# Output product of the last two tokens by tokens on TensorE, with ScalarE's functions grouped and the decay mask on GpSimd, in a hybrid mLSTM and retention block

## The chip, the cores and the metric

The kernel runs on one core of a Trainium2 chip, in one launch. The metric is the device time of that launch in microseconds (us). The engines are named as the profile names them: PE (TensorE's matmuls; PEld its weight loads), DVE (VectorE), ACT (ScalarE), POOL (GpSimd) and SP (SyncE, which issues most DMAs).

## What is computed

One block of a language model over 16 meta tokens and 1024 frames, D = 1024, in f32. A token mixer with eight heads of 256 value columns (four mLSTM heads, four retention heads) is followed by a gated MLP with a causal convolution. Cut to what the change touches:

```python
def token_mixer(u, w_in, ml_conv_w, ml_b_i, ml_b_f, ml_norm_g, rt_norm_g, w_out):
    ...
    qk = jax.nn.silu(causal_dwconv(jnp.concatenate([ml_q, ml_k], axis=-1), ml_conv_w))
    ...
    h_ml = mlstm_chunkwise(to_chunks(q), to_chunks(k), to_chunks(v),
                           to_chunks(li[..., None])[..., 0], to_chunks(lf[..., None])[..., 0])
    h_ml = head_norm(from_chunks(h_ml), ml_norm_g).reshape(b, lp, ML_HEADS * ML_DV)
    h_ml = jax.nn.sigmoid(ml_o.astype(jnp.float32)) * h_ml
    ...
    h_rt = head_norm(from_chunks(h_rt), rt_norm_g).reshape(b, lp, RT_HEADS * RT_DV)
    h_rt = jax.nn.silu(rt_g.astype(jnp.float32)) * h_rt
    mixed = jnp.concatenate([h_ml, h_rt], axis=-1).astype(u.dtype)
    return (mixed @ w_out)[:, n_pad:]
```

In the mLSTM heads a score is weighted with exp(log_d - m_row), where log_d is minus infinity above the diagonal: that is the mask. Four functions of ScalarE alternate: Silu (q and k of mLSTM heads, gate of retention heads), Exp (the decays of mLSTM heads), Sigmoid (gate of mLSTM heads) and Sqrt (the norms).

## The kernel before

Features lie on the 128 partitions and tokens along the free axis, 1040 of them in pieces of 400, 384 and 256 tokens, or in nine chunks (16, then eight of 128) for the scan. Products in the projections are made of three fp32r matmuls each (high by high, high by low, low by high): a weight tile lands by DMA in a raw buffer (two buffers, tag "raw"), ACT casts it to a high part (L151), DVE takes the low part as the rest (L152), and then the buffer is free for the next DMA in the list of units. The order of that list for one head is o (two tiles), m (two tiles of w_out for the last two tokens, of the head before), v (two tiles), q and k of the next head.

The heads run in the order 4, 0, 1, 2, 3, 5, 6, 7 (L1003). For each head the loop merges the gate projections `po` (o_group, L422, three pieces by two halves) with the first chunks of the scan, then the value projections `pv` of the next head (v_group, L358) with the other chunks and the normalisation (post_steps, L872), and then comes the next head's q and k (`pq`, `pk`, qk_group, L395). scan_a (L789) makes the scores and `kwh`, the weighted k for the state update; scan_b (L827) makes the update `u`, the state `C` and the numerator `n`. Before the merged loops of a head, tables (L518) fetches its decays from DRAM into A1 and A2, adds the mask to A1 on DVE (L532, L533) and makes nine Exps on ACT (L536). ACT loads a table (ACT_TABLE_LOAD) whenever the next function is in another set.

The normalised and gated output of a head goes to DRAM (`mxd`), except for the last two tokens of 1040: these go to the small tile mm, since the output stage (class Seven, L579, a scheme with seven half-size products in place of eight, bank names `pwx` and `pwy`) works on 1024 tokens. Their product with w_out is made by last_two (L176) on DVE: for each of the 16 tiles of w_out and each of the two tokens one instruction multiplies the tile with a per-partition value and adds it to acc, 128 partitions by 1024. The sum over partitions is taken much later, in step "4" of the output stage, with 16 matmuls of one column each (L1189), after which DVE adds the result to resid. Sums of weight blocks for the seven products are made by DMAs that add in DRAM (wsum, L188): a first pair on SP's queue (L194), a chain of five on POOL's (L196).

PSUM has eight banks of [128, 512] f32: three "pp", two "sA", one each of "num", "upd" and "tr" (L109). The transposes of post_steps go to "tr", one bank for each half.

The order in which each engine gets its instructions is decided by a scheduler at build time, which may interleave what the program writes one after another; on the chip each engine keeps that order. A call `after(x, y)` adds an edge that only orders x behind y.

## Time and profile before

| | |
|---|---|
| median of 3 runs (lowest, highest) | 1543.4 us (1542.33, 1548.02) |
| the profiled execution's own time | 1549.12 us |
| its span, first to last instruction | 1547.3 us |
| mean granted clock of TensorE | 0.991 |
| heads 4 and 0 to 3, from about | 86 to 500 us |
| heads 5, 6, 7, to about | 742 us |
| output stage (seven products) | 700 to 936 us |
| gated MLP, up and gate, then down | 936 to 1300, 1300 to 1520 us |

A row of a timeline reads: start, duration, engine, line, operation, output tile <- input tiles, shape, and in brackets how long the engine sat idle before it and what ended that. Matmuls are pipelined, so the time that one costs is the step from its start to the next one's start, not its own duration. A granted clock of 0.50 in a stretch means that TensorE ran at half speed there. In the groups of lines the columns behind the bar are busy time, mean duration in ns, and idle time before with what ended it.

### The profile page before, as it was taken

How to read it: one execution, taken by the hardware profiler on the slowest of the kernel's cores; microseconds unless marked ns; L12 is line 12 of the kernel's file. 1: busy time of each engine (PE TensorE's matmuls, PEld its weight loads, DVE VectorE, ACT ScalarE, POOL GpSimd, SP SyncE). 2: the span in 40 equal slices, each digit the busy share in tenths (PEclk: the TensorE clock that was granted, in tenths of full speed). 3: DMA queues.
4: the chain of work that ended last, by engine and by line, in shares of the span. 5: the costliest groups of instructions: out<-in, count | busy, mean ns of one | idle time of the engine just before them, and what ended most of it. 6: DMA issues, size and time to landing. Idle time of an engine off the chain costs nothing.

```text
span 1547.3 us, 25387 instructions
## 1 busy us (share of the span) xinstructions
PE 1524.0 (98%) x9763; PEld 1400.5 (91%) x9763; DVE 1090.0 (70%) x2342; ACT 739.3 (48%) x1494; POOL 90.6 (6%) x109
## 2 busy tenths in 40 slices
PE   8999999999999999999999999999999999999997
PEld 7989999999999999997788998999999999888887
DVE  8757767676867566668867778666666666778657
ACT  7365555555543434336454555444444444434443
POOL 0001000010101000000000000211111110000000
PEclk9999999999999999999999999999999999999999
DMA  6124344262648152347542327888656567923213
GB/s 215 42 70 122 77 123 90 98 142 79 161 111 197 54 128 71 101 111 244 185 137 92 96 94 244 211 223 200 161 145 161 148 156 197 373 99 113 96 41 109
DMA packets 105192, 213.41 MB, mean 138 GB/s; under 512 B 9384, under 2 KB 31600, under 8 KB 105072
## 3 DMA queue, kind: packets, MB, share of 16 engines
q1 hardware_dynamic: 86384, 176.86, 33.6%
q0 software_dynamic: 18544, 34.87, 15.1%
q8 instruction: 76, 1.25, 0.3%
q14 instruction: 44, 0.36, 0.1%
q10 hardware_dynamic: 144, 0.07, 0.0%
HBM read 182.37 MB, written 84.19 MB: 172 GB/s over the span
## 4 chain that ended last, share of the span: by engine, by line
PE 93%; DMA 2%; DVE 2%; ACT 2%; issue 1%; SPq 0%; DVEq 0%; ACTq 0%
PE pv L378 4%; PE pv L379 4%; PE pv L380 4%; PE po L388 3%; PE po L390 3%; PE po L389 3%; PE pdx L554 3%; PE pdx L556 3%; PE pdx L555 3%; PE pup_x L555 2%; PE pup_x L556 2%; PE pga_x L554 2%; PE pga_x L556 2%; PE pga_x L555 2%; PE pup_x L554 2%; PE pwx L555 2%
## 5 line engine op out<-in xcount | busy, mean ns | idle before, releaser
L378 PE MATMUL pv<-hi_v,uh 128*128 128x256 f32 (+1 forms) x512 | 148.3, 290 | 3.1 <-ACT hi_v L151 2.1
L379 PE MATMUL pv<-lo_v,uh 128*128 128x256 f32 (+1 forms) x512 | 147.3, 288 | 0.0
L380 PE MATMUL pv<-hi_v,ul 128*128 128x256 f32 (+1 forms) x512 | 146.2, 287 | 0.0
L388 PE MATMUL po<-uh,hi_o 128*128 128x386 f32 (+2 forms) x384 | 123.9, 323 | 1.1 <-DVE kT L419 1.1
L389 PE MATMUL po<-ul,hi_o 128*128 128x386 f32 (+2 forms) x384 | 122.7, 319 | 0.0
L390 PE MATMUL po<-uh,lo_o 128*128 128x386 f32 (+2 forms) x384 | 122.6, 319 | 0.0
L378 PEld LDWEIGHTS pv<-hi_v,uh 128*128 128x128 f32 x512 | 98.2, 192 | 6.5 <-issue 2.9
L379 PEld LDWEIGHTS pv<-lo_v,uh 128*128 128x128 f32 x512 | 98.2, 192 | 0.8 <-DVE lo_v L152 0.8
L380 PEld LDWEIGHTS pv<-hi_v,ul 128*128 128x128 f32 x512 | 98.1, 192 | 0.1
L245 ACT CAST hi_up<-raw_up 128x512 fp32r<-128x512 f32 (+1 forms) x52 | 36.5, 719 | 107.7 <-PE pga_z L555 60.8
L196 POOL DMA_DIRECT2D wsd<-w_down_d x55 | 50.9, 1025 | 575.0 <-DMA wsd<-w_down_d 482.2
L196 POOL DMA_DIRECT2D wsw<-w_out_d x40 | 37.2, 1028 | 631.2 <-DMA wsw<-w_out_d 593.7
L388 PEld LDWEIGHTS po<-uh,hi_o 128*128 128x128 f32 x384 | 72.3, 188 | 1.4 <-DVE kT L419 1.2
L389 PEld LDWEIGHTS po<-ul,hi_o 128*128 128x128 f32 x384 | 72.3, 188 | 0.1
L390 PEld LDWEIGHTS po<-uh,lo_o 128*128 128x128 f32 x384 | 72.3, 188 | 0.1
L246 DVE TENSOR_TENSOR lo_ga<-fraw_ga,hi_ga 128x512 fp32r<-128x512 f32 (+1 forms) x52 | 41.9, 809 | 38.2 <-ACT hi_ga L245 37.9
L554 PE MATMUL pup_x<-uh_g,hi_up 128*128 128x256 f32 (+1 forms) x240 | 67.2, 282 | 0.4 <-ACT uh_g L1034 0.4
L555 PE MATMUL pup_x<-ul_g,hi_up 128*128 128x256 f32 (+1 forms) x240 | 67.4, 283 | 0.1
L246 DVE TENSOR_TENSOR lo_up<-raw_up,hi_up 128x512 fp32r<-128x512 f32 (+1 forms) x52 | 41.4, 810 | 35.4 <-ACT hi_up L245 34.6
L556 PE MATMUL pup_x<-uh_g,lo_up 128*128 128x256 f32 (+1 forms) x240 | 66.1, 282 | 0.0
L388 PE MATMUL pq<-uh,hi_q 128*128 128x400 f32 (+2 forms) x192 | 62.4, 325 | 0.2 <-DVE rq L409 0.2
L389 PE MATMUL pk<-ul,hi_k 128*128 128x400 f32 (+2 forms) x192 | 62.4, 325 | 0.0
(751 smaller groups left out, 5055.9 us busy)
## 6 DMA issues: line engine op xcount, KB each, us to landing
raw_up<-w_up_d SPq DMA_DIRECT2D x22, 512.0 KB, 6.6
fraw_ga<-w_gate_d SPq DMA_DIRECT2D x22, 512.0 KB, 3.8
acts<-cv SPq DMA_DIRECT2D x44, 256.0 KB, 5.8
wsd<-w_down_d SPq DMA_DIRECT2D x22, 512.0 KB, 7.8
wsd<-w_down_d POOLq DMA_DIRECT2D x22, 512.0 KB, 6.6
rd<-wsd SPq DMA_DIRECT2D x22, 512.0 KB, 3.5
wsd<-w_down_d POOLq DMA_DIRECT2D x33, 256.0 KB, 7.2
raw_o<-w_fm_d SPq DMA_DIRECT2D x16, 512.0 KB, 3.6
```

The source lines that it names most:

```text
L196: nc.gpsimd.dma_start(x, v, accum_op=ALU.add)
L245: nc.scalar.copy(hi[:, o:o + n], x)
L246: nc.vector.tensor_tensor(lo[:, o:o + n], x, hi[:, o:o + n].bitcast(F32), ALU.subtract)
L378: nc.tensor.matmul(pv[:L, :nv], a, hi[:, o:o + nv], start=kb == 0, stop=False)
L379: nc.tensor.matmul(pv[:L, :nv], a, lo[:, o:o + nv], start=False, stop=False)
L380: nc.tensor.matmul(pv[:L, :nv], b, hi[:, o:o + nv], start=False, stop=kb == KB - 1)
L388: nc.tensor.matmul(pt[:, :n], a, uh[kb][:, t0:t1], start=kb == 0, stop=False)
L389: nc.tensor.matmul(pt[:, :n], a, ul[kb][:, t0:t1], start=False, stop=False)
L390: nc.tensor.matmul(pt[:, :n], b, uh[kb][:, t0:t1], start=False, stop=kb == KB - 1)
L554: m.append(nc.tensor.matmul(pt, ah, xh_, start=first and k == 0, stop=False, skip_group_check=True))
L555: nc.tensor.matmul(pt, ah, xl_, start=False, stop=False, skip_group_check=True)
L556: m.append(nc.tensor.matmul(pt, al, xh_, start=False, stop=last and k == n - 1, skip_group_check=True))
```

## The change

1. last_two is called once a head. It takes both w_out tiles of the head, and for each of them and each of four column strips of 256 one f32 matmul: weights mm[h], 128 partitions by 32 columns, of which two are the tokens and 30 zeros; moving data the raw tile. The eight matmuls add up in one "pp" bank, strip j in partitions 32j and up, and DVE adds the bank to acc, now [128, 256]. mm is kept twice, for heads by turns. For head 7 the two tiles are loaded ahead into tiles of their own, and the product follows the last post_steps, in the "num" bank.
2. Two transposes of 128x128 and two additions take the place of the 16 one-column matmuls.
3. Order edges on ACT: Silu of q and k behind the last Sqrt, the decays' Exp behind the last Silu, a Sigmoid gate behind the last Exp, a Silu gate behind the last Sqrt, a Sqrt behind the last gate. The Exps move from tables to a new function decays, called after the q and k groups. ACT's order holds 34 table loads where it held 58.
4. The two mask additions go from DVE to POOL.
5. The last piece's transposes of both halves share one "tr" bank.
6. For mLSTM heads the merge starts the scan one gate group later, and the calls of wsum are spread over other heads.

```diff
-    acc = accp.tile([P, 2, D], F32, name="acc")
-    mm = accp.tile([P, 2 * 8, 2], F32, name="mm")
+    acc = accp.tile([P, D // 4], F32, name="acc")
...
+    mms = [mxp.tile([P, 2, 32], F32, name=f"mm{i}") for i in range(2)]
+    for x in mms:
+        nc.gpsimd.memset(x, 0.0)
+    mm = {h: mms[i % 2] for i, h in enumerate(ORDER)}
...
-    def last_two(k, raw=None):
-        raw = raw_tile(f"m{k}") if raw is None else raw
-        nc.sync.dma_start(raw[:, :D], w_out[k])
-        for t in range(2):
-            if k != 2 * HF:
-                nc.vector.scalar_tensor_tensor(acc[:, t], raw[:, :D], mm[:, k, t:t + 1], acc[:, t], ALU.mult, ALU.add)
-            else:
-                nc.vector.tensor_scalar(acc[:, t], raw[:, :D], mm[:, k, t:t + 1], None, ALU.mult)
+    def last_two(h, raws=None, tag="pp"):
+        if raws is None:
+            raws = [raw_tile(f"m{h}_{b}") for b in range(2)]
+            for b in range(2):
+                nc.sync.dma_start(raws[b][:, :D], w_out[2 * h + b])
+        pt, n = pp(f"two{h}", tag), D // 4
+        for b in range(2):
+            for j in range(4):
+                nc.tensor.matmul(pt[32 * j:32 * j + 32, :n], mm[h][:, b, :], raws[b][:, j * n:(j + 1) * n], start=b == 0, stop=b == 1, tile_position=(0, 32 * j))
+        if h == HF:
+            nc.vector.tensor_copy(acc, pt[:, :n])
+        else:
+            nc.vector.tensor_tensor(acc, pt[:, :n], acc, ALU.add)
...
-            nc.scalar.activation(dst, cv[:, :n], AF.Silu)
+            x = nc.scalar.activation(dst, cv[:, :n], AF.Silu)
+            after(x, last["root"])
+            last["silu"] = x
...
+        x = nc.scalar.activation(s, s, AF.Sigmoid if h < H else AF.Silu)
+        after(x, last["exp"] if h < H else last["root"])
+        last["gate"] = x
...
-        nc.vector.tensor_tensor(a, a, m.rearrange("p (o t) -> p o t", o=1).to_broadcast([P, NCH - 1, P]), ALU.add)
+        nc.gpsimd.tensor_tensor(a, a, m.rearrange("p (o t) -> p o t", o=1).to_broadcast([P, NCH - 1, P]), ALU.add)
+
+    def decays(h):
+        if h >= H:
+            return
         for c in range(NCH):
             t0, L = CH[c]
-            nc.scalar.activation(A1[:, t0:t0 + L], A1[:, t0:t0 + L], AF.Exp, bias=cols[:, 0, c * H + h:c * H + h + 1])
+            x = nc.scalar.activation(A1[:, t0:t0 + L], A1[:, t0:t0 + L], AF.Exp, bias=cols[:, 0, c * H + h:c * H + h + 1])
+            after(x, last["silu"])
+            last["exp"] = x
...
+            x = nc.scalar.activation(z[:, :n], z[:, :n], AF.Sqrt)
+            after(x, last["gate"])
+            last["root"] = x
...
-            tr = ps.tile([P, 512], F32, tag="tr", name=f"tr{h}_{p}_{b}")
+            if b == 0 or p < 2:
+                m["tr"] = ps.tile([P, 512], F32, tag="tr", name=f"tr{h}_{p}_{b}")
+            tr = m["tr"][:, b * (t1 - t0):] if p == 2 else m["tr"]
...
-            for mb in range(KB):
-                for i in range(2):
-                    nc.tensor.matmul(pe[:, 2 * mb + i:2 * mb + i + 1], acc[:, i, mb * P:(mb + 1) * P], cs[:, C_M01 + P - 1:C_M01 + P], start=True, stop=True)
-            V.tensor_tensor(resid[:, :, T - 2:], pe[:, :2 * KB].rearrange("p (m i) -> p m i", i=2), resid[:, :, T - 2:], ALU.add)
+            for i in range(2):
+                nc.tensor.transpose(pe[:, i * P:(i + 1) * P], acc[:, i * P:(i + 1) * P], ident)
+                x = resid[:, i:KB:2, T - 2:]
+                V.tensor_tensor(x, pe[:, i * P:(i + 1) * P].rearrange("p (j t) -> p j t", t=32)[:, :, 0:2], x, ALU.add)
```

What this does to the order is shown at one place, the start of head 1 (in the trace of before from about 326 us), where k of head 1 ends and its gate begins. First PE before, where pk_2 is the last piece of k and po_0_0 the first piece of the gate:

```order
L389 MATMUL pk_2_2991<-ul_85,hi_k_0_2805 128x256
L390 MATMUL pk_2_2991<-uh_84,lo_k_0_2806 128x256
L388 MATMUL po_0_0_3029<-uh_78,hi_o_0_2811 128x386
L389 MATMUL po_0_0_3029<-ul_79,hi_o_0_2811 128x386
L390 MATMUL po_0_0_3029<-uh_78,lo_o_0_2812 128x386
```

And PE after (line numbers from here on are those of the changed kernel, where L388 to L390 are L395 to L397):

```order
L396 MATMUL pk_2_2989<-ul_85,hi_k_0_2803 128x256
L397 MATMUL pk_2_2989<-uh_84,lo_k_0_2804 128x256
L187 MATMUL two_3036<-raw_m_0_3032,mm_94 32x256 x4
L187 MATMUL two_3036<-raw_m_1_3033,mm_94 32x256 x4
L395 MATMUL po_0_0_3046<-uh_78,hi_o_0_2809 128x386
L396 MATMUL po_0_0_3046<-ul_79,hi_o_0_2809 128x386
```

The product of head 0's last two tokens stands between k and the gate, its eight matmuls together; so it does at the start of heads 1, 2, 3, 5, 6 and 7. For head 4 and for head 7 the two fours are apart, with other matmuls between them.

ACT at the same place before, from the first Silu of k to kwh of chunk 0 (hi_v is the cast of the next head's v weights, sig the gate, A_189 the table A1):

```order
L151 CAST hi_v_0_3378<-raw_v_0_3376 128x1024
L415 ACTIVATE kT<-cvk_0_2951 128x400
L431 ACT_TABLE_LOAD
L431 ACTIVATE sig<-sig 128x386
L415 ACT_TABLE_LOAD
L415 ACTIVATE kT<-cvk_1_2985 128x384
L415 ACTIVATE kT<-cvk_2_3019 128x256
L431 ACT_TABLE_LOAD
L431 ACTIVATE sig<-sig 128x384
L806 ACTIVATE kwh_0_3087<-s_0_3083,cols 128x128
```

And after (A_192 is A1):

```order
L422 ACTIVATE kT<-cvk_1_2983 128x384
L154 CAST hi_v_0_3183<-raw_v_0_3181 128x1024
L422 ACTIVATE kT<-cvk_2_3017 128x256
L551 ACT_TABLE_LOAD
L551 ACTIVATE A_192<-A_192,cols 128x16
L551 ACTIVATE A_192<-A_192,cols 128x128 x8
L440 ACT_TABLE_LOAD
L440 ACTIVATE sig<-sig 128x386
L440 ACTIVATE sig<-sig 128x384
L823 ACTIVATE kwh_0_3104<-s_0_3100,cols 128x128
```

The loads between the cast and kwh go from three to two, and all nine Exps now stand between the cast and kwh. The same block stands at the start of heads 0, 2 and 3.

SP's DMA queue at the same place before (wsw are the weight sums, raw_m the w_out tiles for the last two tokens):

```order
L148 DMA raw_o_1_2917<-w_fm_d 128x1024
L194 DMA wsw_1_130<-w_out_d 256x1x512
L920 DMA mxd_95<-sig 128x384
L194 DMA wsw_1_138<-w_out_d 256x1x512
L178 DMA raw_m_3025<-w_out_d 128x1024
L178 DMA raw_m_3164<-w_out_d 128x1024
L920 DMA mxd_94<-sig_176 128x254
L148 DMA raw_v_0_3376<-w_v_d 128x1024
L920 DMA mxd_95<-sig_176 128x254
L148 DMA raw_v_1_3382<-w_v_d 128x1024
```

And after:

```order
L151 DMA raw_o_1_2915<-w_fm_d 128x1024
L183 DMA raw_m_0_3032<-w_out_d 128x1024
L941 DMA mxd_98<-sig 128x384
L183 DMA raw_m_1_3033<-w_out_d 128x1024
L941 DMA mxd_97<-sig_179 128x254
L941 DMA mxd_98<-sig_179 128x254
L151 DMA raw_v_0_3181<-w_v_d 128x1024
L202 DMA wsw_1_133<-w_out_d 256x1x512
L202 DMA wsw_1_141<-w_out_d 256x1x512
L151 DMA raw_v_1_3395<-w_v_d 128x1024
```

The two weight-sum transfers stood ahead of raw_m and now stand between the two halves of raw_v. On POOL's queue the mask additions stand between the five adding DMAs of one weight sum and those of the next, or among them.

More of the change, by code (lines that the diff above doesn't have):

```diff
@@ L204, in u_m @@
     def u_m(h):
-        for b in range(2):
-            units.append((("m", h, b), lambda k=2 * h + b: last_two(k)))
+        units.append((("m", h), lambda h=h: last_two(h)))
     u_v(HF)
@@ L1005, in body @@
         B = lambda c, h=h: ab(h, c)
-        merge([lambda b=b, p=p: (o_group(h, b, p), p == 1 and b and i and wsum_next()) for b in range(2) for p in range(3)],
-              [A(0)] + [B(c) for c in range(4 if h < 7 else NCH)])
+        merge([lambda b=b, p=p: (o_group(h, b, p), p == 1 and b and 0 < i < 6 and wsum_next()) for b in range(2) for p in range(3)],
+              [A(0)] + [B(c) for c in range(4 if h < 7 else NCH)], 1 if h < H else 0)
         if h == 7:
             break
+        if i == 6:
+            wm = [mxp.tile([P, D], F32, name=f"wm{b}") for b in range(2)]
+            for b in range(2):
+                nc.sync.dma_start(wm[b], w_out[14 + b])
         side = post_steps(h, 0) + [B(4), B(5), B(6)] + post_steps(h, 1) + [B(7), B(8)] + post_steps(h, 2)
         nxt = ORDER[i + 1]
-        merge([lambda c=c: (v_group(nxt, c)(), c == 4 and i == 4 and wsum_next()) for c in range(NCH)], side)
+        merge([lambda c=c: (v_group(nxt, c)(), c == 4 and 2 < i < 6 and wsum_next()) for c in range(NCH)], side)
         if i:
@@ L1017, in body @@
                 qk_group(nxt, kind, p)
+        decays(nxt)
     TA, TB = KEEP, KEEP + XW - 2
@@ L1119, in body @@
         run(post_steps(7, p))
+    last_two(7, wm, "num")
     KW = mixw.kn
@@ L1163, in body @@
             mixw.pump()
-        if st == "65" and k == 1:
-            x = fp.tile([P, 4 * XW], F32, name="wm", tag="xh2", bufs=1)
-            last_two(14, x[:, :D])
-            last_two(15, x[:, D:2 * D])
         if st == "1" and k:
```

10 lines of the change are left out of this document (4 added, 6 removed).

## The prediction

> **What bounds the kernel now.** I read the page first, for the share of each engine.
>
> ```profile
> PE 1524.0 (98%) x9763; PEld 1400.5 (91%) x9763; DVE 1090.0 (70%) x2342; ACT 739.3 (48%) x1494; POOL 90.6 (6%) x109
> ```
>
> TensorE (PE) is busy 1524.0 of 1547.3 us, so only 23.3 us of the span can be won by removing idle time; beyond that a gain needs fewer or faster matmuls. DVE and ACT have slack, and their work counts only where PE waits for it. The waits of PE, with total, times and longest, name two large places where DVE or ACT is late:
>
> ```profile
> PE u L823 <- DVE C L861: 2.0, 1, 2.0
> PE u L823 <- ACT kwh L806: 1.8, 1, 1.8
> ```
>
> The table of stretches shows something the busy share hides (columns: us, busy time of PE, PEld, DVE, ACT and POOL with instructions, granted clock, DMA share, GB/s):
>
> ```profile
> 100.73:104.14 3.41, 3.41 (x19) 3.41 (x18) 3.23 (x9) 3.41 (x12) 0.00 (x0) 0.50 0.01 4
> 701.47:704.89 3.42, 3.42 (x13) 2.87 (x12) 2.67 (x7) 3.25 (x5) 0.00 (x0) 0.50 1.02 379
> 834.60:838.01 3.41, 3.41 (x10) 2.64 (x9) 3.03 (x5) 3.41 (x8) 0.00 (x0) 0.50 1.02 382
> ```
>
> In these windows PE counts as busy throughout, at a granted clock of 0.50: each loses about half of 3.41, some 1.7 us. So a stall can be paid twice, as idle time and as a slow window behind it.
>
> **Part by part: the last two tokens (A).** DVE loses these 26 long instructions, two like them and four more for the last head, some 38 us:
>
> ```profile
> L181 DVE SCALAR_TENSOR_TENSOR acc<-raw_m,mm,acc 128x1024 f32<-128x1024 f32 x26 | 32.2, 1278 | 6.5 <-DMA raw_m<-w_out_d 6.3
> ```
>
> PE has to do the product in their place, on the critical engine: eight matmuls per head, 32 columns of weights against 256 columns of f32, in four column strips. Line 367 already does the same form at the start of each v group (PE's rows; one matmul leaves two records, so 16 records are one such group):
>
> ```profile
> 609.22 0.62 PE L367 MATMUL pv<-raw_v,ug 128*32 128x256 f32 x2
> 609.77 0.39 PE L824 MATMUL n<-S_2l,qd_3h 128*128 128x256 f32 x1
> 609.99 0.28 PE L825 MATMUL n<-S_2h,qd_3l 128*128 128x256 f32 x1
> 610.20 1.06 PE L367 MATMUL pv<-raw_v,ug 128*32 128x256 f32 x14
> 611.20 0.39 PE L378 MATMUL pv<-hi_v,uh 128*128 128x256 f32 x1
> ```
>
> From 609.99 to 611.20 one ordinary 256-column matmul (0.12, half of the 0.23 that 512 columns take below) and 14 records take 1.21, so an unbroken group costs about 1.1. Even the short run of two takes 0.55, from 609.22 to 609.77, and the ordinary matmul behind it 0.22 instead of 0.12: each entry and exit costs something of its own. A group broken in two I therefore put at 1.7 (two runs of about 0.85). In the new order six heads have it unbroken, heads 4 and 7 in two halves: 6 x 1.1 + 2 x 1.7 = **+10.0**. Nothing hides it. The eight additions of 128x256 that DVE gets instead are noise.
>
> **The one-column matmuls (B, C).** Before, 16 matmuls of one column stood in the output stage:
>
> ```profile
> 828.46 0.39 PE L554 MATMUL pwx<-rr,w4xh 128*128 128x512 f32 x1
> 828.69 4.54 PE L1189 MATMUL pe<-cs,acc 128*128 128x1 f32 x32
> 833.09 0.77 PE L555 MATMUL pwx<-rr,w4xh 128*128 128x512 f32 x1
> 837.93 0.44 PE L554 MATMUL pwx<-rr,w4xh 128*128 128x512 f32 x1
> ```
>
> From 828.69 to 833.09 they take 4.4; the two 128x128 transposes in their place I price at 0.2 together: **-4.2**. Behind them, from 833.09 to 837.93, eleven 512-column matmuls take 4.84 instead of 11 x 0.23 = 2.53 (0.23 is the step from 828.46 to 828.69): the clock is at 0.50 there. PE's queue was never empty, so that the one-column stretch brings the slow windows on is my inference, from their place; I count **-2.2**, and 0 as the other end.
>
> **The mask on GpSimd (D).** DVE's row first, then PE's:
>
> ```profile
> 98.50 1.23 DVE L533 TENSOR_TENSOR A<-A,mask 128x1024 f32<-128x1024 f32 x1 [4.45 <-DMA A<-scr]
> ```
>
> ```profile
> 97.86 0.28 PE L378 MATMUL pv<-hi_v,uh 128*128 128x256 f32 x1
> 100.12 0.39 PE L823 MATMUL u<-vh,kwh 128*128 128x256 f32 x1 [1.97 <-DVE C L861]
> ```
>
> DVE stood 4.45 us in front of the mask, whose table was still arriving, and the copy C that PE needed, as PE's row says, was queued behind it. On GpSimd the mask blocks no one on DVE: -2.0, and the slow window at 100.73 that follows the stall, -1.7: **-3.7**. GpSimd itself is slower: its only elementwise rows are
>
> ```profile
> 1541.03 1.40 POOL L1495 TENSOR_TENSOR resid<-resid,Rb 128x256 f32<-128x256 f32 x2 [245.02 <-ACT Rb L313]
> ```
>
> so 0.70 per 256 columns and 2.8 for the 1024. Queued behind it there are the adding DMAs of the weight sums, needed only after 740 us; who waits for it are the Exps, which the change moves past the k group, tens of us later. No cost, and if that cover were gone, 2.8 - 1.2 = 1.6 per head.
>
> **ScalarE's groups (E).** ACT's rows at the start of head 1, then PE's:
>
> ```profile
> 332.41 1.05 ACT L151 CAST hi_v<-raw_v 128x1024 fp32r<-128x1024 f32 x1 [10.83 <-DMA raw_v<-w_v_d]
> ...
> 336.59 1.28 ACT L415 ACT_TABLE_LOAD   x1
> 337.89 0.83 ACT L415 ACTIVATE kT<-cvk 128x384 f32<-128x384 f32 x2
> ...
> 340.03 0.52 ACT L431 ACTIVATE sig<-sig 128x384 f32<-128x384 f32 x1
> 340.46 0.35 ACT L806 ACTIVATE kwh<-s,cols 128x128 fp32r<-128x128 f32 x1
> ```
>
> ```profile
> 326.31 0.34 PE L388 MATMUL po<-uh,hi_o 128*128 128x386 f32 x1
> 337.84 0.38 PE L793 MATMUL s<-qT,kT 128*128 128x128 f32 x2
> 338.70 0.33 PE L388 MATMUL po<-uh,hi_o 128*128 128x386 f32 x1
> 340.86 0.39 PE L823 MATMUL u<-vh,kwh 128*128 128x258 f32 x1 [1.83 <-ACT kwh L806]
> ```
>
> The cast waited for the weights of the next v, and three loads (the one at 336.59 and one on each side of it) stood between it and kwh: PE lost some 2.0 here, from 338.70 to 340.86. The loads go from 58 to 34; that frees 24 x 1.28 = 31 us of ACT, of which PE was waiting for these 2.0: **-2.0**. The Trainium skill (ScalarE: Activation LUTs, What ACT_TABLE_LOAD costs) has about 2.66 us for a change of set, with a drain. The load at 336.59 is followed by work at 337.89, so here a change costs 1.30, and the trace doesn't agree. By that page's figure each chain below, with two loads, would end 2.7 later, and the sum would be some 11 us worse.
>
> What comes in its place is the new order of ACT at the start of heads 0 to 3: cast of v, Silu of the last piece of k, load, nine Exps, load, two Sigmoids, kwh. One row gives the Exps:
>
> ```profile
> 388.18 2.46 ACT L536 ACTIVATE A<-A,cols 128x128 f32<-128x128 f32 x8 [0.50 <-DVE A L533]
> ```
>
> Cast 1.05, Silu 0.42 (half of the two at 337.89), load 1.28, Exps 2.46 and about 0.3 for the short one, load 1.28, two Sigmoids of 0.52, kwh 0.35 make 8.2; start to start such rows overlap a little, so I take 7.9 from the landing of raw_v to the end of kwh. The buffer for raw_v comes free when the first half of the new product has run: raw tiles have two buffers, and both hold w_out rows. That is about 0.65 after the product starts. The times from issue to landing of raw_v and of raw_m are
>
> ```profile
> DMA to landing us min/median/max: 3.5/4.9/7.6
> DMA to landing us min/median/max: 3.6/7.2/10.2
> ```
>
> PE comes to u after the product (1.1), the 72 matmuls from 326.31 to 337.84 (11.5) and the scores (0.25): 12.9. So it waits for (landing - 4.35): nothing at 3.5, 0.55 at the median, 3.25 at 7.6. I take the median, since the same transfer is meant, at four boundaries: **+2.2** (0 to +13).
>
> PE now also waits for raw_m itself, where DVE did before:
>
> ```profile
> 656.57 0.87 SPq L178 DMA_DIRECT2D raw_m<-w_out_d  x1
> 665.38 0.34 PE L388 MATMUL po<-uh,hi_o 128*128 128x386 f32 x1
> ```
>
> The second half of the product would start at about 665.38 + 0.65, 9.5 after the issue; the longest landing is 10.2: **+0.7** (0 to +3).
>
> **Rest (G, H).** In head 7's k group DVE stood in front of the same transfer, and kT came late (DVE's row, then PE's); -1.1, as the long instruction is gone. Two stalls at 740 us are those of PE on the single bank for transposes (PE's rows); with both halves in one bank I count them away, -1.6, though the bank's next user may still wait:
>
> ```profile
> 666.84 2.48 DVE L181 SCALAR_TENSOR_TENSOR acc<-raw_m,mm,acc 128x1024 f32<-128x1024 f32 x2 [4.63 <-DMA raw_m<-w_out_d]
> ```
>
> ```profile
> 671.10 0.44 PE L388 MATMUL po<-uh,hi_o 128*128 128x384 f32 x1 [1.06 <-DVE kT L419]
> 740.03 0.41 PE L901 MATMUL tr<-cs,A 128*128 128x128 f32 x2 [0.79 <-DVE mm L908]
> 741.23 0.47 PE L554 MATMUL pwy<-wtq,hi_w 128*128 128x512 f32 x1 [0.80 <-DVE mm L908]
> ```
>
> The weight sums are issued at other places; nothing waits for them before the output stage: 0.
>
> **Sum.** 10.0 - 4.2 - 2.2 - 3.7 - 2.0 + 2.2 + 0.7 - 1.1 - 1.6 = -1.9. The profiled execution took 1549.1 (span 1547.3), so 1547.2 in its terms; the median of the runs, 1543.4, lies 5.7 below it, which gives 1541.5.
>
> **Rivals.** *Late weights (slower).* The new SP order puts two 512 KB weight-sum transfers right behind raw_v, as they stand before raw_m now; if raw_v then takes raw_m's 7.2, PE waits 2.85 at four boundaries, 11.4 instead of 2.2, and if two of them are followed by a slow window (the stall at 97.86 was, the one at 338.70 wasn't), 3.4 more: 1541.5 + 12.6 = 1554. It decides from a landing of about 6.5 on. For it speaks raw_m's median, against it that raw_v goes first in the queue. 14%.
>
> *GpSimd and DVE in each other's way.* If a mask held DVE up for its whole 2.8, at a place like 97.86, four would cost 11.2: 1552.7. The trace has one pair side by side, at 1541, and DVE's instructions there aren't seen to stop. 4%. The Trainium skill (SBUF — State Buffer, Who interferes with whom) says that a DVE instruction with two SBUF inputs and a GpSimd one that reads SBUF exclude each other; no run here shows it.
>
> *The stalls only move.* D, E, G and H are repaid by the next late wait; A, B and C remain: +3.6, 1547. For it speaks that PE's waits are short and that something is nearly late behind each. 20%.
>
> *More goes than I count.* Raw_v lands early (-2.9 with raw_m's term), and with DVE freer at the end of head 7 the slow window at 701.47 goes too (-1.7), and as much again in stalls under 1 us that I don't list: 1535. DVE's 38 us speak for it, the 23 us of idle time against. 24%.
>
> **Numbers.** Forecast 1541.5 with 38%. Half a per cent, 7.7 us, is about what a measurement of this kernel can tell from no change. Its own range is 1536 to 1549, from C, H and the landings. The range of 1531 to 1552 takes in the other cases but the worst of late weights and of the gains. Faster by over 7.7: most of the last rival and a little of the forecast, 0.24. Slower: most of the first two, 0.15. Within: 0.61.
>
> **What would show it.** Right: the one-column stretch at 828 and the half clock behind it gone, no wait of u on C near 98, eight new PE groups of 1.1 to 1.7, ACT loads down by 24. Wrong: waits of u on kwh over 2 us at the start of heads 0 to 3, PE waiting on raw_m, half-clock windows at new places, or groups of the product far from 1.1.

## The result and the profile after

The changed kernel takes 1555.95 us in the median, the kernel before 1544.1 on the same chip: a ratio of 1.0069 [1.005, 1.0089], so slower by 0.7%. The forecast of 1541.5 was 14.4 too low, and its range ended at 1552. The profile shown here is that of a second set of runs of the changed kernel (e1_after, e1 for short; span 1553.8, own time 1555.56), because the first profiled execution ran at a granted clock of 0.848.

The page of the changed kernel, its share of the engines:

```profile
PE 1527.0 (98%) x9861; PEld 1397.2 (90%) x9861; DVE 1058.7 (68%) x2311; ACT 709.7 (46%) x1470; POOL 101.5 (7%) x119
```

DVE lost 31 us of work and ACT 30, as the change means it; PE's own busy time rose by 3.0. Where the span grew is read from fixed points in PE's order, the first matmul of a group in each kernel. First the changed kernel's `po` of head 7 and `pup_x`, which ends the output stage:

```profile
669.39 0.44 PE L395 MATMUL po<-uh,hi_o 128*128 128x386 f32 x1
...
927.61 0.28 PE L571 MATMUL pup_x<-uh_g,hi_up 128*128 128x256 f32 x1
```

And the same `pup_x` in the kernel before (its `po`, at 665.38, stands in the prediction):

```profile
922.35 0.28 PE L554 MATMUL pup_x<-uh_g,hi_up 128*128 128x256 f32 x1
```

| stretch of PE's order | before | changed | difference | what the prediction's terms give for it |
|---|---|---|---|---|
| to `po` of head 7 | 665.38 | 669.39 | +4.01 | 8.3 (A without head 7) - 3.7 - 2.0 + 2.2 + 0.7 = +5.5 |
| `po` of head 7 to `pup_x` | 256.97 | 258.22 | +1.25 | 1.7 - 4.2 - 2.2 - 1.1 - 1.6 = -7.4 |
| the rest of the MLP | 624.9 | 626.2 | +1.26 | 0 |

The second row is where the forecast broke: from the last head's gate to the end of the output stage it expected 7.4 us less and got 1.25 more. PE's waits in the changed kernel say what it stands on there (total, times, longest); all three lie between 717 and 760 us, and none of them is in the list of before:

```profile
PE n L840 <- DVE C L882: 2.6, 1, 2.6
PE pwx L571 <- ACT hi_w L252: 2.0, 2, 1.6
...
PE n L841 <- DVE S_7l L803: 1.4, 1, 1.4
```

PE's rows at this place in the changed kernel, the last chunks of the last scan:

```profile
717.16 0.28 PE L842 MATMUL n<-S_6h,qd_7l 128*128 128x256 f32 x1
720.06 0.58 PE L840 MATMUL n<-vh,pt_8h 128*128 128x256 f32 x1 [2.62 <-DVE C L882]
...
722.73 0.58 PE L841 MATMUL n<-S_7l,qd_8h 128*128 128x256 f32 x1 [1.44 <-DVE S_7l L803]
...
724.95 0.79 PE L571 MATMUL pwx<-rr,hi_w 128*128 128x512 f32 x1 [0.46 <-ACT hi_w L252]
```

Before, the same two matmuls of the scan, `n<-S_6h` and `n<-vh,pt_8h`, lie 5.67 us apart, and PE works through all of it, on the first weights of the output stage:

```profile
717.41 0.28 PE L825 MATMUL n<-S_6h,qd_7l 128*128 128x256 f32 x1
...
722.16 1.08 PE L554 MATMUL pwx<-rr,hi_w 128*128 128x512 f32 x4
723.08 0.28 PE L823 MATMUL n<-vh,pt_8h 128*128 128x256 f32 x1
```

The filler is gone from the changed kernel's order. And the stalls are paid twice: its table of stretches (columns as in the prediction) has three windows of half clock in a row, of which these are the first and the last:

```profile
719.76:723.17 3.41, 1.66 (x6) 1.37 (x6) 3.41 (x10) 1.20 (x3) 0.00 (x0) 0.50 0.12 43
...
726.59:730.00 3.41, 3.41 (x11) 2.65 (x10) 1.41 (x7) 1.30 (x3) 0.00 (x0) 0.50 0.47 156
```

Why the filler is gone is read from SP's queue, first of the changed kernel and then of before:

```profile
669.09 0.81 SPq L241 DMA_DIRECT2D raw_up<-w_up_d  x2
675.04 10.66 SPq L618 DMA_DIRECT2D raw_w<-w_out_d  x2
...
716.05 10.76 SPq L618 DMA_DIRECT2D raw_w<-w_out_d  x2
```

```profile
659.50 0.38 SPq L601 DMA_DIRECT2D raw_w<-w_out_d  x1
...
669.34 13.68 SPq L601 DMA_DIRECT2D raw_w<-w_out_d  x3
...
732.86 0.33 SPq L234 DMA_DIRECT2D raw_up<-w_up_d  x1
```

raw_up is the first weight of the MLP, which PE needs some 200 us later. Before, it is fetched at 732.86, after the four tiles raw_w of the output stage (659.5 to 683). Now it goes first, at 669.09, and the raw_w come at 675 to 686 and 716 to 727. ACT's cast and DVE's subtraction split a weight tile and so free its raw buffer. The casts show why the new order hurts (count, durations in ns, first and last start), in the changed kernel

```profile
L252 ACT CAST hi_w<-raw_w x8: 1032/1047/1054, 682.8 to 758.2; 128x1024 fp32r<-128x1024 f32 x8
...
L252 ACT CAST hi_up<-raw_up x2: 1047/1050/1053, 672.7 to 826.2; 128x1024 fp32r<-128x1024 f32 x2
```

and before

```profile
L245 ACT CAST hi_w<-raw_w x8: 1032/1048/1055, 667.4 to 742.0; 128x1024 fp32r<-128x1024 f32 x8
```

Of the two raw_up that take both raw buffers at 669, one is split at 672.7 and the other at 826.2. The second holds one of the two buffers for 157 us, and the eight raw_w go through the other alone: the first is split 15.4 us later than before, the last 16.2.

The change brings that about in a line that the diff under "The change" leaves out, in the list of units:

```diff
-        for b in range(2):
-            units.append((("m", h, b), lambda k=2 * h + b: last_two(k)))
+        units.append((("m", h), lambda h=h: last_two(h)))
```

The gate asks for its weights with `need(("o", h, b), 2)` (L426 before, L435 now): issue the units up to this one and two further. Behind the second o unit these two were m and m. With one m unit a head they are m and the next thing in the list: the first half of the next v in heads 0 to 3, 5 and 6 (head 4, the first, has no m), and the MLP's first weights in head 7.

### The profile page after: what moved, and what is told of

It reads as the page before. It is cut to its first block, busy times and chain, and to the rows that moved or that the text cites. A ratio compares the mean times of both kernels' runs of the same rounds, so it can differ in the third digit from the quotient of the medians.

```text
span 1657.0 us, 25551 instructions
## 1 busy us (share of the span) xinstructions
PE 1634.7 (99%) x9861; PEld 1465.6 (88%) x9861; DVE 1064.9 (64%) x2311; ACT 710.4 (43%) x1470; POOL 102.5 (6%) x119
## 3 DMA queue, kind: packets, MB, share of 16 engines
q8 instruction: 77, 1.26, 0.3%
## 4 chain that ended last, share of the span: by engine, by line
PE 95%; DVE 2%; ACT 1%; DMA 1%; issue 0%; DVEq 0%; SPq 0%; ACTq 0%
PE pv L385 4%; PE po L395 4%; PE pv L387 4%; PE po L397 4%; PE pv L386 4%; PE po L396 4%; PE pdx L572 3%; PE pdx L573 3%; PE pdx L571 3%; PE pga_x L571 2%; PE pga_x L573 2%; PE pup_x L572 2%; PE pga_x L572 2%; PE pup_x L573 2%; PE pup_x L571 2%; PE pdy L572 2%
## 5 line engine op out<-in xcount | busy, mean ns | idle before, releaser
L385 PE MATMUL pv<-hi_v,uh 128*128 128x256 f32 (+1 forms) x512 | 154.3, 302 | 2.7 <-ACT hi_v L154 1.7
L386 PE MATMUL pv<-lo_v,uh 128*128 128x256 f32 (+1 forms) x512 | 151.9, 297 | 0.0
L387 PE MATMUL pv<-hi_v,ul 128*128 128x256 f32 (+1 forms) x512 | 151.6, 297 | 0.0
L395 PE MATMUL po<-uh,hi_o 128*128 128x386 f32 (+2 forms) x384 | 129.9, 338 | 0.0
L397 PE MATMUL po<-uh,lo_o 128*128 128x386 f32 (+2 forms) x384 | 128.2, 334 | 0.0
L396 PE MATMUL po<-ul,hi_o 128*128 128x386 f32 (+2 forms) x384 | 127.8, 333 | 0.0
L385 PEld LDWEIGHTS pv<-hi_v,uh 128*128 128x128 f32 x512 | 102.6, 200 | 6.7 <-issue 3.3
L386 PEld LDWEIGHTS pv<-lo_v,uh 128*128 128x128 f32 x512 | 102.5, 200 | 0.8 <-DVE lo_v L155 0.8
L395 PEld LDWEIGHTS po<-uh,hi_o 128*128 128x128 f32 x384 | 74.5, 194 | 4.3 <-issue 2.4
L397 PEld LDWEIGHTS po<-uh,lo_o 128*128 128x128 f32 x384 | 74.3, 193 | 0.4
L439 DVE TENSOR_TENSOR sig<-po,Rb 128x386 f32<-128x386 f32 (+2 forms) x48 | 24.6, 513 | 71.9 <-PE po L397 71.9
L395 PE MATMUL pq<-uh,hi_q 128*128 128x400 f32 (+2 forms) x192 | 65.3, 340 | 0.2 <-DVE rq L416 0.2
L395 PE MATMUL pk<-uh,hi_k 128*128 128x400 f32 (+2 forms) x192 | 65.3, 340 | 0.0
```

Of the source, the lines that this page charges most:

```text
L385: nc.tensor.matmul(pv[:L, :nv], a, hi[:, o:o + nv], start=kb == 0, stop=False)
L386: nc.tensor.matmul(pv[:L, :nv], a, lo[:, o:o + nv], start=False, stop=False)
L387: nc.tensor.matmul(pv[:L, :nv], b, hi[:, o:o + nv], start=False, stop=kb == KB - 1)
L395: nc.tensor.matmul(pt[:, :n], a, uh[kb][:, t0:t1], start=kb == 0, stop=False)
L396: nc.tensor.matmul(pt[:, :n], a, ul[kb][:, t0:t1], start=False, stop=False)
L397: nc.tensor.matmul(pt[:, :n], b, uh[kb][:, t0:t1], start=False, stop=kb == KB - 1)
```

## The experiments

Each kernel was timed beside the kernel before on the same chip. Since the median of before lies between 1544.1 and 1546.5 from one such set of runs to the next, comparisons are made by the ratios, each with its 95% interval; 0.1% is 1.5 us. The expectations number the theories in the order in which I came to them.

| run | what it is | median us | ratio to before |
|---|---|---|---|
| e1_after | the changed kernel again | 1555.9 | 1.0065 [1.005, 1.0081] |
| e2_no_product | changed, product back on DVE | 1540.9 | 0.9973 [0.9962, 0.9984] |
| e3_no_groups | changed, no edges on ACT, Exps back in tables | 1575.18 | 1.0191 [1.0177, 1.0205] |
| e4_product_alone | before with the product on PE | 1563.27 | 1.0112 [1.0096, 1.0128] |
| e5_reach_7 | changed, look-ahead one unit shorter in head 7 | 1546.69 | 1.0012 [1.0001, 1.0023] |
| e6_before_reach | before, look-ahead one unit longer in head 7 | 1560.17 | 1.0102 [1.0086, 1.0118] |
| e7_own_tiles | changed, w_out rows in tiles of their own | 1558.46 | 1.0085 [1.0064, 1.0105] |
| e8_no_last | changed, without head 7's product | 1553.23 | 1.0053 [1.0035, 1.007] |
| e9_no_edges | e5 without the edges | 1568.44 | 1.0142 [1.0122, 1.0161] |
| e10_mask_dve | e5 with the mask on DVE | 1549.88 | 1.0024 [1.0015, 1.0034] |
| e11_product_reach | e4 with e5's look-ahead | 1550.94 | 1.0033 [1.0021, 1.0045] |
| e12_strip_sum | e2, the 16 one-column matmuls replaced | 1545.38 | 0.9988 [0.9977, 0.9999] |
| e13_no_edges_dve | e9 with the mask on DVE | 1550.89 | 1.0027 [1.0016, 1.0039] |
| e14_strip_same | e12 in one bank | 1544.84 | 0.9992 [0.9982, 1.0001] |
| e15_no_product_again | e2 again | 1541.95 | 0.9968 [0.9956, 0.998] |
| e16_mask_alone | before with the mask on POOL | 1543.06 | 0.9989 [0.9975, 1.0003] |
| e17_reach_no_edges | e9, look-ahead of before in all heads | 1552.65 | 1.0047 [1.0034, 1.0059] |
| e18_reach_all | changed, look-ahead of before in all heads | 1548.92 | 1.002 [1.001, 1.0031] |

**Which part costs: e1 to e4.** e1 has no edit. e2 takes the product out and keeps the rest; e3 takes ScalarE's grouping out; e4 is the product alone in the kernel before. Their cores:

```diff
e2 -        units.append((("m", h), lambda h=h: last_two(h)))
e2 +        for b in range(2):
e2 +            units.append((("m", h, b), lambda k=2 * h + b: last_two(k)))
e3 -            after(x, last["root"])
e3 -        after(x, last["exp"] if h < H else last["root"])
e3 -            after(x, last["silu"])
e3 -            after(x, last["gate"])
e4 -            units.append((("m", h, b), lambda k=2 * h + b: last_two(k)))
e4 +        units.append((("m", h), lambda h=h: last_two(h)))
```

> The changed kernel again, for an undisturbed trace: 1554 to 1557 us, about 12 over the kernel before. Theory 1 (late weights, the recorded rival): PE waits for kwh at the start of heads 0 to 3, some 10 us in all, with half-clock windows behind. Theory 2 (the product's own price): no such waits; PE's idle time is about as before or less, and the product with its disturbance of the matmuls around it costs more than the 10 us that the prediction counted, while the stalls that were to go were worth less. Theory 3 (GpSimd and DVE exclude each other): DVE instructions beside a mask on POOL last over 2 us.

> The changed kernel with the product of the last two tokens on DVE and the 16 one-column matmuls as before; ScalarE's groups, the mask on GpSimd, the shared bank and the moved weight sums stay. Theory 1: little changes at the boundaries but raw_v comes free from DVE again; 1548 to 1556. Theory 2: the loss goes, 1540 to 1546. Theory 3: stays at 1552 or above.

> The changed kernel without the order edges on ScalarE and with the Exps back in tables, right behind the mask. Theory 1: the waits at the starts of heads go, 1543 to 1548. Theory 2: 1553 to 1560, since the product stays. Theory 3: 1552 or above.

> The kernel before with nothing but the product on TensorE and the two transposes in place of the one-column matmuls. By the prediction's terms A, B, C: +3.6 on the kernel before, 1547 to 1549. Theory 1: 1545 to 1549. Theory 2: 1550 to 1558. Theory 3: 1545 to 1549.

All the loss comes with the product: without it the rest of the change is 0.27% faster than before, and alone it costs 1.12%, some 17 us, where its own terms (A, B, C) come to 3.6. That ACT's grouping is worth 1.3% (e3 against e1) I had not expected; I come back to it.

**The look-ahead: e5 to e8.** The theory that came from SP's queue, against the rivals that the w_out rows hold the raw buffers too long for PE (e7 gives them tiles of their own and keeps the look-ahead) and that the last product is in the way of the output stage (e8 leaves out head 7's part of the last two tokens).

```diff
e5 -        U = need(("o", h, b), 2)
e5 +        U = need(("o", h, b), 1 if h == 7 and b else 2)
e6 -        U = need(("o", h, b), 2)
e6 +        U = need(("o", h, b), 3 if h == 7 and b else 2)
e7 -            raws = [raw_tile(f"m{h}_{b}") for b in range(2)]
e7 +            raws = [mxp.tile([P, D], F32, name=f"wm{h}_{b}", tag=f"wm{b}", bufs=1) for b in range(2)]
e8 -    last_two(7, wm, "num")
```

> The changed kernel with the look-ahead of the last head's second gate half one unit shorter, so that the first weights of the MLP are no longer fetched in front of the output stage. New theory 4 (look-ahead): one unit a head in place of two lets the list of units reach the MLP's first weights 60 us too early; they hold a raw buffer through the start of the output stage, its own weights come one by one, and PE has nothing to put between the last scan chunks. Then the waits at 717 to 725 us and the half-clock stretch behind them go: 1544 to 1547. Theory 2 (the product itself costs more than counted): 1553 to 1557.

> The kernel before, its product on DVE and all else untouched, with the look-ahead of the last head's second gate half one unit longer. Theory 4: raw_up is issued near 665 us instead of 733, raw_w comes late, and the kernel before loses what the changed one lost at that place: 1552 to 1558. Theory 2: nothing changes, 1543 to 1547.

> The changed kernel with two tiles of their own for the w_out rows of the last two tokens, so that the product holds no raw buffer; the look-ahead stays, so the MLP's first weights still come early. Theory 4: no gain, 1553 to 1557, raw_up still near 669. A rival form of it (it is raw_m that holds the buffers until PE reaches the product): 1544 to 1548.

> The changed kernel without the product of the last head (that head's part of the last two tokens is left out). Theory 4: it saves its own eight matmuls, 1.3 to 1.7, and the stalls at 717 to 725 stay: 1553 to 1555. Rival (the product in front of the output stage makes the order bad there): 1544 to 1548.

e5 brings 0.53% back, 8 us, with one unit fewer at one place. SP's queue in e5 has the order of before again:

```profile
669.77 16.59 SPq L618 DMA_DIRECT2D raw_w<-w_out_d  x4
...
734.35 0.33 SPq L241 DMA_DIRECT2D raw_up<-w_up_d  x1
```

The three waits above are gone from its list, it has no half clock between 39 and 1537 us, and the stretch from `po` of head 7 to `pup_x` takes 248.8, which is 8.2 less than before. e6 puts the same fault into the kernel before and loses 1.02%, more than I had expected. Its SP queue and the top of PE's waits:

```profile
658.17 0.33 SPq L234 DMA_DIRECT2D raw_up<-w_up_d  x1
...
711.00 9.31 SPq L601 DMA_DIRECT2D raw_w<-w_out_d  x2
```

```profile
PE pwx L554 <- ACT hi_w L245: 6.2, 2, 4.6
```

So the early raw_up is the cause in both directions. e7, where the first raw_up goes out at 649.03, gains nothing (1.0085), and e8 only 0.12 to 0.16% (some 2 us; the product itself takes 1.3): both rivals fall.

**What is left of each part: e9 to e14.** With the look-ahead mended, e9 takes the edges away, e10 the mask from POOL, e11 is e4 mended. e12 and e14 test whether e2, the fastest so far, would gain from losing the one-column stretch alone.

```diff
e9 -            after(x, last["root"])
e9 -        after(x, last["exp"] if h < H else last["root"])
e9 -            after(x, last["silu"])
e9 -            after(x, last["gate"])
e10, e13 -        nc.gpsimd.tensor_tensor(A1[:, :META], A1[:, :META], m[:, :META], ALU.add)
e10, e13 +        nc.vector.tensor_tensor(A1[:, :META], A1[:, :META], m[:, :META], ALU.add)
e11 +        U = need(("o", h, b), 1 if h == 7 and b else 2)
e12 -            for mb in range(KB):
e12 -                for i in range(2):
e12 -                    nc.tensor.matmul(pe[:, 2 * mb + i:2 * mb + i + 1], acc[:, i, mb * P:(mb + 1) * P], cs[:, C_M01 + P - 1:C_M01 + P], start=True, stop=True)
e12 +            for i in range(2):
e12 +                for j in range(4):
...
e12 +            pe = pp("pe3", "num")
e14 -            pe = pp("pe3", "num")
```

> The changed kernel with the shorter look-ahead of e5 and without the order edges on ScalarE; the Exps stay behind the q and k groups. It holds 52 table loads against 34. If the grouping itself is worth the 18 loads of 1.28 us, 1565 or above; if, as the prediction's term E has it, only a load on PE's way counts, 1546 to 1550. The loss of e3 came, by its trace, from an Exp that waits for a mask queued behind the weight sums on POOL; with the Exps late it must not come back.

> The changed kernel with the shorter look-ahead of e5 and the mask back on DVE. By term D of the prediction the stall near 98 us comes back, 2.0, with or without a half-clock window of 1.7 behind it: 1548 to 1551. If the mask on POOL is worth nothing where it stands, 1545 to 1548.

> The kernel before with the product on TensorE and the two transposes alone, as e4, and with the shorter look-ahead. Theory 4 takes the same 9 to 15 us off e4: 1547 to 1553, and the prediction's A, B and C (+3.6) are then what is left, 1548. If the product alone costs more than that, 1552 or above.

> A version meant to beat both: e2, with the product on DVE, but the sum over partitions made with eight column-strip matmuls of 256 columns and four transposes in place of the 16 one-column matmuls. The strips cost 1.1 as one product group does, the transposes some 0.5, against 4.4 and the half clock behind it: 2.8 to 5 us under e2, 1536 to 1538. If the half-clock window there has another cause, 1538 to 1539.

> As e12, with the four transposes in the bank of the strip sums instead of a second one. If the stalls at 857 to 862 us that ate e12's gain come from the bank taken from the next users, they go, and it is 2 to 4 us under e2's time on the same chip; otherwise it equals e12.

e11 says that the product as such costs 0.33%, 5 us; without the mend it was 1.12%. e10 is 0.12% above e5, with intervals that overlap: the mask on POOL is worth some 2 us, perhaps nothing. e9 loses 1.3%, 20 us, though it has only 18 more table loads (52 against 34 in ACT's order). That is the size I had put on the loads, but the trace names the cause that I had ruled out. Its largest wait, with four places:

```profile
PE n L837 <- ACT num L871: 13.4, 4, 7.0
```

The first of the two long ones, PE and then ACT and POOL of e9:

```profile
270.50 0.58 PE L837 MATMUL n<-vh,pt_1h 128*128 128x258 f32 x1 [5.16 <-ACT num L871]
```

```profile
260.70 1.28 ACT L549 ACT_TABLE_LOAD   x1
267.71 0.31 ACT L549 ACTIVATE A<-A,cols 128x16 f32<-128x16 f32 x1 [5.72 <-POOL A L541]
...
270.09 0.36 ACT L871 COPY num<-n 16x257 f32<-16x257 f32 x1
```

```profile
253.65 1.05 POOL L204 DMA_DIRECT2D wsw<-w_out_d  x1 [29.54 <-DMA wsw<-w_out_d]
260.17 1.94 POOL L204 DMA_DIRECT2D wsw<-w_out_d  x2 [5.47 <-issue]
266.60 0.83 POOL L204 DMA_DIRECT2D wsw<-w_out_d  x1 [4.49 <-DMA wsw<-w_out_d]
267.14 0.53 POOL L541 TENSOR_TENSOR A<-A,mask 128x16 f32<-128x16 f32 x1
```

It is no matter of the loads. The small piece of the mask stands on POOL behind four of the five adding DMAs of a weight sum, the fourth of which waits for an earlier one to land; ACT's Exp waits 5.72 for the mask, num is behind that in ACT's queue, and PE waits 5.16 for num. Two windows of half clock come with it, from 268.9 to 275.8. The same happens near 360 us, with 7.0. With the edges the scheduler puts the Exps elsewhere, and in the changed kernel PE's longest wait for num is 0.8.

e12 takes 16 one-column matmuls out of e2 and is not faster: 0.9988 against 0.9973. PE's waits between 740 and 925 us in e12 are

```profile
PE pup L565 <- DVE xl L1053: 2.2, 1, 2.2
PE pga L564 <- ACT hi_ga L245: 0.8, 1, 0.8
PE pwy L564 <- ACT Rb L313: 0.7, 1, 0.7
PE prb L309 <- ACT Rb L311: 0.3, 1, 0.3
```

and e15, the same kernel with the stretch, has none in that time. So 4.0 us of waits eat what B and C bring; e14 shows that the bank isn't the reason. Why the scheduler's order got worse there stays open.

**Why the queue is late: e13, e15 to e18.**

```diff
e16 -        nc.vector.tensor_tensor(A1[:, :META], A1[:, :META], m[:, :META], ALU.add)
e16 +        nc.gpsimd.tensor_tensor(A1[:, :META], A1[:, :META], m[:, :META], ALU.add)
e17 -        U = need(("o", h, b), 1 if h == 7 and b else 2)
e17 +        U = need(("o", h, b), 2 - b)
e18 -        U = need(("o", h, b), 2)
e18 +        U = need(("o", h, b), 2 - b)
```

e13 is e9 with e10's edit, e15 is e2 once more.

> As e9 (shorter look-ahead, no order edges on ScalarE, Exps late), but with the mask on DVE. Theory 5 (POOL's queue): e9's 22 us over e5 are Exps that the order puts early on ACT and that wait there for a 16-column mask queued on POOL behind the weight sums' DMAs, with the numerator's copies queued behind the Exp. Then the loss goes with the mask's queue: 1548 to 1553. Rival (the 18 table loads themselves cost it): it stays at 1562 or above.

> The kernel of e2 again, beside the others on one chip: 0.3% under the kernel before.

> The kernel before with nothing but the mask on POOL; the Exps stay in tables, with no edges. The prediction's term D alone: 3.7 under the kernel before. Theory 5: the Exps wait on POOL's queue at the starts of heads 1 and 2, as in e3 and e9: 10 to 25 us over it.

> As e9 (no order edges on ScalarE, mask on POOL), but with the look-ahead of every head's second gate half one unit shorter. Theory 6: it is again the look-ahead that puts the weight sums behind raw_v on SP, 29 us later than in e16, so that their chain on POOL stands in front of the 16-column mask. With the old reach the chain is through in time and the loss of e9 goes with the edges still out: 1547 to 1553. Rival (the moved weight sums or the later start of the scan put it there): 1562 or above.

> The changed kernel, edges and all, with the look-ahead of every head's second gate half one unit shorter. If the edges already keep the Exps out of the way, this equals e5: 1545 to 1548.

e13 wins back 1.15% of e9's loss, so the mask's place on POOL is the price there; but e16, the mask alone in the kernel before, loses nothing (0.9989), where I had expected a loss of the same kind. POOL's rows in e16 show the same chain, done earlier:

```profile
224.70 1.06 POOL L196 DMA_DIRECT2D wsw<-w_out_d  x1 [6.69 <-DMA wsw<-w_out_d]
...
252.62 0.22 POOL L534 TENSOR_TENSOR A<-A,mask 128x16 f32<-128x16 f32 x1 [7.36 <-DMA A<-scr]
```

There the mask waits for its own table and not for the chain. The chain begins 29 us later in e9, since the pair on SP that it adds to is issued later. SP's queue in e16 and then in e9:

```profile
219.53 1.22 SPq L194 DMA_DIRECT2D wsw<-w_out_d  x2
```

```profile
247.64 0.33 SPq L151 DMA_DIRECT2D raw_v<-w_v_d  x1
248.03 1.22 SPq L202 DMA_DIRECT2D wsw<-w_out_d  x2
```

In the code that pair is ordered behind the last raw transfer (`after(..., last["raw"])`, L202), and with the longer look-ahead that is the first half of the next v, which waits for a raw buffer. e17 tests this: the look-ahead of before in all heads (in the first, which has no m, one unit shorter), no edges, mask on POOL. Most of the loss goes (1.0142 to 1.0047), and the chain is again through, from 229.56 to 249.65, when the small piece of the mask comes:

```profile
257.90 0.22 POOL L541 TENSOR_TENSOR A<-A,mask 128x16 f32<-128x16 f32 x1 [7.44 <-DMA A<-scr]
```

It is the same one unit of look-ahead as in head 7, with another victim. e18, the whole change with the look-ahead of before everywhere, is at 1.002, no better than e5. The best version is the change without the product: e2 and e15, at 0.9973 and 0.9968, beat both kernels.

## Why the prediction failed, step by step

**The step that failed** is the list of units. The prediction counted the weight sums as "nothing waits for them before the output stage: 0" and gave the merging of two m units into one no term at all. It read SP's order at the start of head 1, where raw_v moves ahead, and not at head 7, where the same shift brings raw_up ahead of raw_w. Of the 14.4 us, 8.4 are in the sum (span against span +6.5 instead of -1.9): 8.65 in the table's second row, while the other two nearly cancel (of the MLP's 1.26, 0.8 is PE's wait for uh_g in `pup_x`, 1.2 instead of 0.4; the rest stays open). e5 shows the second row to be this step: with the look-ahead mended it comes to -8.2, against the -7.4 of the terms. That it comes so near is partly luck: before's profiled execution spent 10.24 us of this stretch at half clock (from 701.48 and from 831.18, some 5.1 lost), e5 none, and the terms have 2.2 for that.

**The second step that failed** is the translation, the other 6.0. I took 5.7 off because before's profiled execution (1549.1) was slower than its runs, but e1's own time of 1555.56 was its median within 0.4, and no reason had carried the deduction over to the new kernel. The excess goes with half clock. That execution had it at five places ahead of the last 10 us, e1 at two and e15 at one; and of the 100 executions of before that were timed beside the experiments, the five with its granted clock, 0.991, took 1549.3 in the mean, the 23 with 0.996 took 1544.3. The sum had already taken off some of these windows (1.7 in D, 2.2 in C), so up to 3.9 of the 5.7 was taken off twice. So even without the fault the forecast would have been missed: e5, with 1.0012, is 2 us above before and not 2 below. That is what the rival of the stalls that only move gave (1547 against 1546.69).

**A, the product, was right.** One unbroken group in the changed kernel, at the place of the prediction's order rows:

```profile
327.00 0.28 PE L397 MATMUL pk<-uh,lo_k 128*128 128x256 f32 x1
327.21 1.07 PE L187 MATMUL two<-raw_m,mm 128*32 128x256 f32 x16
328.21 0.44 PE L395 MATMUL po<-uh,hi_o 128*128 128x386 f32 x1
```

From 327.00 to 328.21 less one 256-column matmul of 0.12 is 1.09, against 1.1. The six heads with an unbroken group have 1.10 to 1.12 more from q to the gate. The broken groups of heads 4 and 7 are two runs of 0.57 each (156.83 to 157.40 and 162.33 to 162.90 for head 4); with the slower step of a neighbour that is some 1.3 instead of 1.7. In all A comes to 9.2 instead of 10.0.

**B and C, the one-column stretch, went as said in the changed kernel and can't be had alone.** The stretch and the half clock behind it are gone in all kernels without it. That the stretch brings the window on was called an inference. For it: before, e2, e6 and e15 have the stretch and a window that begins in the stretch or within 1 us of its end, and none of the kernels without it has a window between 783 and 930 us. Against it: e16 has the stretch, at 824.8, and no window. So it is likely, not necessary. e12 shows the gain given back in waits.

**D, the mask, has the right sign, and its gain and its cover were priced wrongly.** In the changed kernel there is no wait of u on C near 98 and no window at 100.73; from `po` of head 4 to the next `pq` takes 63.9 instead of 66.2. But most of that is the window, and the window isn't bound to the stall: e6, e10 and e11 have the stall (2.0 to 2.3, at 98 to 100) and none behind it, and e6, which at this place is the kernel before, takes 64.7. And PE now waits at the next u, for another input:

```profile
102.55 0.36 PE L840 MATMUL u<-vh,kwh 128*128 128x256 f32 x1 [1.63 <-ACT vh L360]
```

POOL's row has 2.39, where the prediction had 2.8:

```profile
98.02 2.39 POOL L544 TENSOR_TENSOR A<-A,mask 128x1024 f32<-128x1024 f32 x1 [9.90 <-PE n L842]
```

By e10 and e16 the mask on POOL is worth some 2 us instead of 3.7, with intervals that also allow nothing. And "if that cover were gone, 2.8 - 1.2 = 1.6 per head" named the duration of the mask, and the price is the queue that it stands in: 5.2 and 7.0 at two places in e9, and 6.8 and 10.2 us at half clock behind them. The DMAs that the prediction itself named on that queue were the term.

**E, ScalarE's groups, was right for what it counted.** Head 1's stretch from gate to the next q takes 60.0 instead of 62.4, -2.4 against -2.0. With the mask on DVE the edges are worth next to nothing (e13 against e10: 0.03%), with the mask on POOL and the look-ahead of before 0.27% (e17 against e18), and 1.3% where they keep ACT clear of POOL's late queue. So 18 loads, 23 us of ACT by the 1.28 of the row at 260.70 above, lie beside PE's work but for 0.5 to 4.2 us, as the prediction read them.

**The rival of late weights did not happen.** SP, ACT and PE of the changed kernel at head 1:

```profile
327.92 0.33 SPq L151 DMA_DIRECT2D raw_v<-w_v_d  x1
```

```profile
331.45 1.05 ACT L154 CAST hi_v<-raw_v 128x1024 fp32r<-128x1024 f32 x1 [3.34 <-DMA raw_v<-w_v_d]
...
338.94 0.35 ACT L823 ACTIVATE kwh<-s,cols 128x128 fp32r<-128x128 f32 x1
```

```profile
340.88 0.28 PE L840 MATMUL u<-vh,kwh 128*128 128x258 f32 x1
```

The transfer lands 3.5 after its issue, at the lower end of the rows quoted, kwh is done 1.6 ahead of u, and the term of +2.2 is 0. That of raw_m (+0.7) is 0 too, since all eight matmuls of head 6's product stand ahead of `po` without a wait (in e17 and e18 one group waits 0.7 and 0.2 for raw_m).

**POOL and DVE do get in each other's way, but PE doesn't wait for it.** "On GpSimd the mask blocks no one on DVE" is wrong, and the runs show what the prediction had seen in none. DVE and then POOL of the changed kernel:

```profile
217.38 2.95 DVE L155 TENSOR_TENSOR lo_k<-raw_k,hi_k 128x1024 fp32r<-128x1024 f32 x1 [1.21 <-ACT hi_k L154]
```

```profile
216.84 2.41 POOL L544 TENSOR_TENSOR A<-A,mask 128x1024 f32<-128x1024 f32 x1 [31.95 <-DMA A<-scr]
```

lo_k, which reads two tiles in SBUF, begins beside the mask and ends 1.08 after it. It takes 2.95, the sign that theory 3 of e1 named, where in e10, with the mask on DVE, all eight lo_k take 1.21 to 1.23. It is so again at 302.70 (2.21), and at three places of e16 (2.3 to 2.7). So at these places DVE loses 1.0 to 1.7 to a mask that took 1.23 of its own time. PE has no wait between 216 and 233 in the changed kernel, and e16 as a whole is at 0.9989: the 11 us of the second rival did not come, since lo_k isn't what PE waits for there.

**G and H.** The wait of `po` on kT at 671 is gone (G). H moved: e5 still waits 0.7 for mm at the last transposes, which is one of the two stalls counted away.

## What to carry to other kernels

When a change merges or splits the entries of a prefetch list, count again what "two further" reaches at every place, above all at the last pass of a loop, where the next entry belongs to another stage: here one entry too far held one of two buffers for 157 us and cost 8 to 16 us. An operation that is moved to an engine with free time takes the place of that engine's queue, and its price is the wait at its position, not its duration; nor does it leave the old engine alone, if both then read at once. And a deduction from a profile to a median needs a reason that holds for the new kernel too.

## What the runs showed of the hardware

- Windows of half clock last 3.41 us or two or three times that, but for the one at the end of each trace (8.2 in before). Some begin at a stall of PE (2.62 up to 720.06 in e1, window from 719.76; 5.16 up to 270.50 in e9, window from 268.94), some at a stretch of one-column matmuls in which PE never waits (822.5 to 826.1 in e2, window from 825.8). Others of the same kind bring none (the stall of 2.34 up to 100.40 in e10, the stretch at 824.8 in e16). At a granted clock of 0.50 they lose about half their length.
- How many such windows an execution has differs from one to the next: the granted clock of the kernel before lay between 0.990 and 0.998, and its time between 1541 and 1550.
- The five adding DMAs of one weight sum, the later ones of which wait for earlier ones to land, take 17 to 20 us on POOL's queue from the first to the last (253.65 to 270.97 in e9, 224.70 to 244.44 in e16), and a vector operation behind them waits with them (267.14 in e9).
- An elementwise instruction of 128x1024 on POOL and one on DVE that both read two tiles in SBUF don't run side by side: the one on DVE ended 1.1 us after POOL's at all five places above, and in e5 POOL's took 3.10 instead of 2.40 behind one of DVE (389.12).
- An f32 group of eight matmuls in four column strips of 32 costs 1.1 us in one piece and some 1.3 in two (327.21 and 162.33 in e1).
